# Splitting a pair's weight pieces in their order of use, with one sum formed a step earlier from raw weights

## The chip, the cores and the metric

The kernel runs on one core of a Trainium2 chip. What counts is the device time of one execution in microseconds (us), as the median of several runs. The engines carry short names here: PE (TensorE, the matmuls), PEld (its weight loads), DVE (VectorE), ACT (ScalarE), POOL (GpSimd) and SP (SyncE, which here issues the loads of the weights). Each engine works through its own stream of instructions in order, and an instruction that waits on a semaphore holds up all that stand behind it on that engine.

## The reference

The program is a two-layer trunk over 512 frames of width 1024. Cut to the products that matter here, one layer is:

```python
h = rmsnorm(x, norm1_g[i])
z = h @ w_in[i] + b_in[i]                       # q, k, v, o of the mLSTM; rq, rk, rv, rg; gates gm, gr
...
merged = jax.nn.sigmoid(gm) * (y_m @ w_bm[i]) + jax.nn.sigmoid(gr) * (y_r @ w_br[i])
x = x + merged @ w_out[i]
h2 = rmsnorm(x, norm2_g[i])
x = x + jnp.square(jax.nn.relu(h2 @ w_ff1[i] + b_ff1[i])) @ w_ff2[i] + b_ff2[i]
```

All weights are float32 in memory and each is used once, so the kernel is a stream of weights past a resident activation.

## The kernel before

**Splitting.** A float32 matmul is made of three faster ones: weights and activations are each split into a high part `h` and a low part `l`, and a product is formed as h·h + h·l + l·h (the weight's part named first: L557 weight high with activation high, L558 weight high with activation low, L559 weight low with activation high). For each piece of weights of 128 x 1024 numbers ACT makes the high part (a copy at L321) and DVE the low part (a subtraction at L322 that reads ACT's result). The row `w_B<-wr` on ACT is thus the high part of piece B, and `w_B<-wr,w_B` on DVE the low one; `wr` is the raw piece as loaded.

**Pairs.** 75 of the units of weights are "pairs": the rotary projections of the retention (`brq`, `brk`, four heads a layer), two of the four gate blocks `bgm`, the four `gr`, and most of the two feed-forward products (`f` and `o`). A pair computes a 2 x 2 block product by seven products instead of eight (Strassen's scheme in Winograd's form). Each product is 12 matmuls of 256 columns. The weights of a pair come as four pieces, each with its own high and low part:

- A holds B11 and t1, and feeds P1 and P5
- B holds B21 and t2, and feeds P6 and P2
- C holds B22 and t3, and feeds P3 and P7
- D holds t4 alone (half the width), and feeds P4

`run_pair` issues them in the order P1, P5, (P4 of the pair before), P6, P2, P3, P7; its own P4 is put off into the next unit. So the order of use is A, A, B, B, C, C, D. Three PSUM banks a, b, c collect the products: P1, P6, P7, P4 go one after the other into bank a, P5 and P3 into c, P2 into b. After each product an eviction reads the bank, and the next product into the same bank waits for it. Where the pair's result goes through `pair_tiles`, ACT evicts P1, P5, P6 and P4 (L633, L635, L639, L645), and DVE adds P2, P3 and P7 (L637, L641, L643). In the second feed-forward product `o` the evictions are DVE adds into `l0x` or `l1x` (L1554, L1556).

**Sums of the weights.** t1, t3 (and in some pairs t2 and t4) are formed beforehand by additions in DRAM, by DMAs that POOL issues (L379). 28 pairs, 14 in each layer (the brq, brk, bgm and gr pairs), have no such t2: DVE forms it as t1 + B22, from the second half of A's raw piece and the first half of C's, into the second half of B's raw buffer. This is the sum of L481. Pairs that are not "full" form t4 as well: DVE adds the two halves of B's raw piece into its own buffer (L484), and the split of D reads it there. Hence B's raw buffer is in use until D has been split.

**Order of preparation.** `PIECE` lists the pieces, and the list gives the order in which they are loaded and split. `ready(k)` calls `prep_next` until piece k is prepared, some pieces ahead of its use. `prep_next` first tops up the raw loads (`fill_raws`, on SP's queue, in order, into four buffers and one extra), then splits one piece. In program order the old list gives A, C, B, D. The sum of L481 stands behind the split of C, the sum of L484 behind the split of B. The split pieces live in a ring of three buffers (tag `w`) and D in one of its own; a split waits until the matmuls that read the buffer's last content are over. A scheduler, by priorities and by when data is due, then decides how the instructions of an engine's stream interleave, but the splits and the loads keep their order among themselves (`in_order`).

Of the kernel before, what the change touches and what calls it, by code (L numbers as in the profile page):

```python
# [38 lines left out]
OP = mybir.AluOpType  # L39
# [6 lines left out]
D = 1024  # L46
# [4 lines left out]
Q = 512  # L51
# [42 lines left out]
PRODUCTS = {"P1": ("A", 0, 0), "P5": ("A", 1, 4), "P2": ("B", 0, 2), "P6": ("B", 1, 5), "P3": ("C", 0, 6),  # L94
            "P7": ("C", 1, 3), "P4": ("D", 0, 1)}

PIECE = {"A": ("B11", "t1"), "C": ("B22", "t3"), "B": ("B21", "t2"), "D": ("t4",)}

GIVEN = ("B11", "B12", "B21", "B22")
MADE = {"t1": ("B12", "B11"), "t3": ("B12", "B22"), "t2": ("t1", "B22"), "t4": ("t2", "B21")}  # L100
# [15 lines left out]
def parts_of(u):  # L116

    return {"PAIR": list(PIECE), "WIDE": HALVES}.get(u[0], [0])

# [5 lines left out]
def is_wide(g):  # L125
    return g[1][:2] in ("rv", "rw")


def is_full(g):

    return is_gate(g) or g[0] > 0 and g[1][0] == "f"


def has_t2(g):

    return is_full(g) or g[1][0] == "f"
# [117 lines left out]
def build(ctx, tc, ins, out):  # L254
    nc = tc.nc
    ve, ac, gp, te = nc.vector, nc.scalar, nc.gpsimd, nc.tensor
    units = [u for i in range(L) for u in unit_list(i)]
# [59 lines left out]
    def tmp(name, dt=F32):  # L317
        return cur["tmp"].tile([P, T], dt, name=name, tag="t", bufs=cur["ntmp"])

    def split(src, hi_ap, lo_ap):  # L320
        a = ac.activation(hi_ap, src, AF.Copy)  # L321
        return a, ve.tensor_sub(lo_ap, src, hi_ap.bitcast(F32))  # L322

    def in_order(kind, *new):

        for a, b in zip(cur.get(kind, ()), new):
            tc.add_manual_dep(b.ins, a.ins.name, ORDER, reason="order of the weights")
        cur[kind] = new
# [4 lines left out]
    for g, v in groups().items():  # L333
        index[g] = len(index)
        src, n, w = ("wwide", 2, UN) if is_wide(g) else ("wpairs", len(v), Q)
# [7 lines left out]
    def block(g, x):  # L343
        return given[g, x] if x in GIVEN else sums[g, x]
# [54 lines left out]
    def full(n):  # L399
        return units[n][0] in ("PAIR", "WIDE") and is_full(units[n][1])  # L400

    order = [(n, x) for n, u in enumerate(units) for x in parts_of(u)]
    place = {x: k for k, x in enumerate(order)}
    loads = [(n, x) for n, x in order if full(n) or x not in ("D", ("t4", 0), ("t4", 1))]
    raws, pieces, kept = {}, {}, {}
    formed = {}

# [3 lines left out]
    def halves(n):  # L411

        return [slice(0, Q), slice(Q, UN)] if n == 1 else [slice(0, UN)]

    def fill_raws(most=RAWS + 1):
        while at["load"] < len(loads) and len(raws) + len(kept) < most:
            n, x = loads[at["load"]]
            r = None
            if n in cur["room"] and cur["more"] not in raws:
                cur["more"] = n, x  # L420
                r = cur["low"].tile([P, UN], F32, name=f"wr{at['load']}", tag="wrx", bufs=1)
            elif len(raws) - (cur["more"] in raws) >= RAWS:
                break
            raws[n, x] = r = r or wpool.tile([P, UN], F32, name=f"wr{at['load']}", tag="wr", bufs=RAWS)
            if x:
                _, g, p = units[n]
                assert made.get((g, x[1] if is_wide(g) else p)) == 2 * len(MADE_OF(g)), (g, p, made, at["unit"])
                if is_wide(g):
                    in_order("load", nc.sync.dma_start(r, block(g, x[0])[x[1]]))
                else:  # L430
                    for k, y in enumerate(PIECE[x][:1] if x == "B" and not has_t2(g) else PIECE[x]):
                        in_order("load", nc.sync.dma_start(r[:, k * Q:(k + 1) * Q], block(g, y)[p]))
            elif units[n][0] == "IF":
                eng = nc.sync if n else nc.scalar
                eng.dma_start(r[:, 0:64], ins["wif"][n * L // NU])
            else:
                w = ins["wstream"][at["whole"]]
                for c in halves(n):
                    in_order("load", nc.sync.dma_start(r[:, c], w[:, c]))
                    for k in (2, 3) if n == 1 and not c.start else ():  # L440
                        nc.sync.dma_start(cur["x0"][k], ins["xT"][k])
                at["whole"] += 1
            at["load"] += 1

    def prep_next():
        n, x = order[at["prep"]]
        at["prep"] += 1
        fill_raws()

        w = Q if x == "D" else UN  # L450
        pl = cur["last"] if n >= NU - LAST else wpool
        kw = {"tag": "d", "bufs": 1} if x == "D" else {"tag": "l", "bufs": LAST} if pl is not wpool else {
            "tag": "w", "bufs": PIECES}
        wide = isinstance(x, tuple)
        nm = f"{x[0]}{x[1]}" if wide else x
        gates = units[n][0] == "IF"
        both = pl.tile([P, 2 * w + SLACK], F32R, name=f"w{n}_{nm}", **kw)
        o = 22 if units[n][0] == "PAIR" or pl is not wpool else 0
        out_ = [both[:, o + a * w:o + a * w + w] for a in range(1 if gates else 2)]
        r = formed.pop((n, x), None)  # L460
        if r is None:
            r = raws.pop((n, x))
        if gates:
            z = out_[0]
            gp.memset(z.bitcast(F32), 0.0)
            z = z.rearrange("p (k g c) -> p k g c", g=4, c=32)
            split(r[:, 0:64].rearrange("p (k g c) -> p k g c", g=2, c=H), z[:, :, 0:2, 0:H], z[:, :, 2:4, 0:H])
        elif x == 0:
            with tc.high_priority(AHEAD if n < 10 and units[n][0] == "V" or units[n][1:] == SOON else 0):
                for c in halves(n):  # L470
                    in_order("prep", *split(r[:, c], *[a[:, c] for a in out_]))
        else:
            in_order("prep", *split(r[:, :w], *out_))
        pieces[n, x] = out_
        if full(n) or not wide and x in ("A", "C") and has_t2(units[n][1]):
            pass
        elif x == "A" or wide and x[0] == "t2":
            kept[n, x] = r
        elif x == "C":

            ve.tensor_tensor(raws[n, "B"][:, Q:], kept.pop((n, "A"))[:, Q:], r[:, :Q], OP.add)  # L481
        elif x == "B":

            ve.tensor_tensor(r[:, :Q], r[:, :Q], r[:, Q:], OP.add)  # L484
            formed[n, "D"] = r
        elif wide and x[0] == "B21":
            t = cur["br"].tile([P, UN], F32, name=f"t4{n}_{x[1]}", tag=("ph", "pl")[x[1]])
            ve.tensor_tensor(t, kept.pop((n, ("t2", x[1]))), r, OP.add)
            formed[n, ("t4", x[1])] = t

    def ready(k):
        while at["prep"] < min(len(order), k + 1):
            prep_next()
# [44 lines left out]
    def run_pair(name, act, done):  # L538
# [5 lines left out]
        def product(x):  # L544
            w, half, j = PRODUCTS[x]
            ready(place[n, "A"] + READY[x])
            wh, wl = [a[:, half * Q:(half + 1) * Q] for a in pieces[n, w]]
            b = {"P2": "b", "P5": "c", "P3": "c"}.get(x, "a")
            first = x in ("P1", "P5") or x == "P2" and "b" not in bank
            if first:  # L550
                bank[b] = own(f"{name}{b}") if x == "P2" and cur["own"] else ps(f"{name}{b}")
            o = bank[b][:, 0:S]
            for k in range(4):
                s = slice(k * P, (k + 1) * P)
                h, l = act[k](j)
                f, e = first and k == 0, k == 3
                te.matmul(o, wh[:, s], h, start=f, stop=False, skip_group_check=True)  # L557
                te.matmul(o, wh[:, s], l, start=False, stop=False, skip_group_check=True)  # L558
                cur["mm"] = te.matmul(o, wl[:, s], h, start=False, stop=e, skip_group_check=True)  # L559
            if x == "P1" and cur["own"] == "written":  # L560
                bank["b"] = own(f"{name}b")
                with ahead():
                    ac.activation(bank["b"][:, 0:S], o, AF.Copy)
            else:
                done(x, o)
            if x == "P2" and cur["own"]:
                cur["own"] = "written"
            pace()

        def last():  # L570
            product("P4")
            for w in PIECE:
                del pieces[n, w]
# [404 lines left out]
    def big(name, dt):  # L978

        return [bpool.tile([P, T], dt, name=f"{name}{k}", tag="big", bufs=KT) for k in range(KT)]  # L980

    x = big("x0", F32)
# [25 lines left out]
    for i in range(L):  # L1008
# [440 lines left out]
        for c in range(KT):  # L1449
# [4 lines left out]
            u = tmp(f"l{i}bml{c}")  # L1454
# [15 lines left out]
        if i == L - 1:  # L1470
            x_pool = phase("x", act_side)
            whole = x_pool.tile([P, KT, T], F32, name=f"l{i}x", tag="x")
            x = [whole[:, c, :] for c in range(KT)]
        else:
            x = big(f"l{i}x", F32)
# [361 lines left out]
```

## Time and profile before

| | |
|---|---|
| median of three runs | 2280.92 us (2279.55 to 2281.22) |
| the profiled execution's own time | 2280.06 us |
| its span | 2278.3 us |
| granted TensorE clock in it | 0.999 |
| DVE busy | 1747.5 us (77 %) |
| ACT busy | 1281.5 us (56 %) |

The page of a profile lists busy times by engine, the chain of work that ended last, and groups of instructions. The view of waits sums, for each engine and line, the idle time just before its instructions and names what ended it. The timeline lists single instructions with start, duration and, in square brackets, idle time with its releaser. Matmuls are pipelined: their ends are modelled (0.28 or 0.39 us each), while the next one of 256 columns starts 0.11 to 0.12 us later. So what a wait costs PE is read from the starts: the step between two starts, less that 0.11. The names of tiles have their numbers left out (`w_B` is piece B of any unit), while the listings of order below carry them: `w43_B` is piece B of unit 43.

### The profile page before, as it was taken

Reading aid. Unit: us, or ns where it says so; the run is one execution under the profiler, and the core shown is the slowest. Engines: PE = TensorE matmul, PEld = TensorE weight load, DVE = VectorE, ACT = ScalarE, POOL = GpSimd, SP = SyncE. Lnnn points to the kernel's source line nnn. Section 1 sums busy time; section 2 is a strip of 40 time slices with the busy share of each in tenths; the row PEclk is TensorE's granted clock in tenths of the full one; section 3 lists DMA queues with packets and bytes.
Section 4 is the critical chain, followed back from the end, with each engine's and each line's share of the span. In section 5 each row is a group of like instructions: output and inputs, shape, how many; then the busy total and the mean of one; then the engine's idle time right before and its main releaser. Section 6 shows DMA issues by size and latency. Waiting matters only on the chain.

```text
span 2278.3 us, 36390 instructions
## 1 busy us (share of the span) xinstructions
PE 2263.4 (99%) x13532; PEld 2009.3 (88%) x13532; DVE 1747.5 (77%) x2680; ACT 1281.5 (56%) x1881; POOL 605.5 (27%) x952
## 2 busy tenths in 40 slices
PE   9999999999999999999999999999999999999998
PEld 8888899888898899999888888998888988999997
DVE  7877777886676877787779687678867678887786
ACT  6766544654554556556557564455545546566564
POOL 3332222223124322223432322221231243111112
PEclk9999999999999999999999999999999999999999
DMA  6776887787789888888787768877877898888841
GB/s 215 189 192 176 246 224 223 222 232 216 236 231 267 222 229 228 238 238 222 227 220 197 185 178 244 240 210 223 239 216 219 248 265 217 256 239 231 249 159 60
DMA packets 185889, 499.32 MB, mean 219 GB/s; under 512 B 26400, under 2 KB 26784, under 8 KB 185712
## 3 DMA queue, kind: packets, MB, share of 16 engines
q0 software_dynamic: 57520, 188.53, 37.0%
q1 hardware_dynamic: 112496, 280.57, 36.6%
q10 hardware_dynamic: 15696, 27.91, 3.6%
q8 instruction: 106, 1.74, 0.3%
q14 instruction: 71, 0.58, 0.1%
HBM read 478.03 MB, written 194.51 MB: 295 GB/s over the span
## 4 chain that ended last, share of the span: by engine, by line
PE 90%; DVE 5%; ACT 2%; issue 1%; DMA 1%; POOL 0%; SPq 0%; DVEq 0%; ACTq 0%; POOLq 0%
PE l0f L502 2%; PE l0f L503 2%; PE l0f L504 2%; PE l0br L502 1%; PE l0br L503 1%; PE l1br L502 1%; PE l1br L503 1%; PE l1br L504 1%; PE l0br L504 1%; DVE w_B L322 1%; PE l0pg L502 1%; PE l0pg L504 1%; PE l1bm L503 1%; PE l0bm L503 1%; PE l0bm L502 1%
## 5 line engine op out<-in xcount | busy, mean ns | idle before, releaser
L322 DVE TENSOR_TENSOR w<-wr,w 128x1024 fp32r<-128x1024 f32 (+1 forms) x193 | 234.3, 1217 | 47.6 <-ACT w L321 45.3
L321 ACT ACTIVATE w<-wr 128x1024 fp32r<-128x1024 f32 (+1 forms) x193 | 199.7, 1041 | 122.3 <-issue 28.5
L321 ACT ACTIVATE w_B<-wr 128x1024 fp32r<-128x1024 f32 x123 | 130.5, 1061 | 148.5 <-PE l1bm L504 13.1
L322 DVE TENSOR_TENSOR w_B<-wr,w_B 128x1024 fp32r<-128x1024 f32 x123 | 150.2, 1222 | 52.5 <-ACT w_B L321 52.3
L321 ACT ACTIVATE w_C<-wr 128x1024 fp32r<-128x1024 f32 x75 | 79.3, 1058 | 63.4 <-issue 9.5
L322 DVE TENSOR_TENSOR w_C<-wr,w_C 128x1024 fp32r<-128x1024 f32 x75 | 92.5, 1234 | 28.6 <-ACT w_C L321 28.6
L322 DVE TENSOR_TENSOR w_A<-wr,w_A 128x1024 fp32r<-128x1024 f32 x75 | 91.7, 1223 | 15.6 <-ACT w_A L321 14.6
L321 ACT ACTIVATE w_A<-wr 128x1024 fp32r<-128x1024 f32 x75 | 79.0, 1053 | 39.6 <-DMA wr<-wpairs 8.8
L321 ACT ACTIVATE w_t<-wr 128x1024 fp32r<-128x1024 f32 x56 | 59.4, 1060 | 62.7 <-PE l0g2va L610 6.3
L321 ACT ACTIVATE w_D<-wr 128x512 fp32r<-128x512 f32 x75 | 47.3, 631 | 67.3 <-DVE wr L484 18.3
L322 DVE TENSOR_TENSOR w_t<-wr,w_t 128x1024 fp32r<-128x1024 f32 x56 | 68.3, 1222 | 21.2 <-ACT w_t L321 20.6
L502 PE MATMUL l0f<-l0n2h,w 128*128 128x512 f32 x176 | 68.8, 391 | 0.0
L503 PE MATMUL l0f<-l0n2l,w 128*128 128x512 f32 x176 | 68.7, 390 | 0.0
L504 PE MATMUL l0f<-l0n2h,w 128*128 128x512 f32 x176 | 68.6, 390 | 0.0
L322 DVE TENSOR_TENSOR w_D<-wr,w_D 128x512 fp32r<-128x512 f32 x75 | 51.7, 689 | 14.1 <-ACT w_D L321 13.7
L379 POOL DMA_DIRECT2D s30t<-wpairs x24 | 16.8, 701 | 88.7 <-PE l1o20a L559 8.7
L504 PEld LDWEIGHTS l0f<-l0n2h,w 128*128 128x128 f32 x176 | 33.1, 188 | 6.9
L502 PEld LDWEIGHTS l0f<-l0n2h,w 128*128 128x128 f32 x176 | 33.1, 188 | 6.6
L503 PEld LDWEIGHTS l0f<-l0n2l,w 128*128 128x128 f32 x176 | 33.1, 188 | 6.5
L502 PE MATMUL l1f<-l1n2h,w 128*128 128x512 f32 x96 | 37.6, 392 | 0.0
L503 PE MATMUL l1f<-l1n2l,w 128*128 128x512 f32 x96 | 37.5, 390 | 0.0
L504 PE MATMUL l1f<-l1n2h,w 128*128 128x512 f32 x96 | 37.4, 390 | 0.0
(5828 smaller groups left out, 9081.2 us busy)
## 6 DMA issues: line engine op xcount, KB each, us to landing
wr<-wstream SPq DMA_DIRECT2D x189, 512.0 KB, 5.0
wr<-wpairs SPq DMA_DIRECT2D x225, 256.0 KB, 4.0
wr<-wwide SPq DMA_DIRECT2D x48, 512.0 KB, 4.6
s3t<-wwide POOLq DMA_DIRECT2D x24, 256.0 KB, 4.3
s6t<-wwide POOLq DMA_DIRECT2D x24, 256.0 KB, 5.2
s18t<-wwide POOLq DMA_DIRECT2D x24, 256.0 KB, 5.6
s21t<-wwide POOLq DMA_DIRECT2D x24, 256.0 KB, 5.1
s24t<-wpairs POOLq DMA_DIRECT2D x24, 256.0 KB, 5.8
```

The lines of the kernel that those rows point to most:

```text
L321: a = ac.activation(hi_ap, src, AF.Copy)
L322: return a, ve.tensor_sub(lo_ap, src, hi_ap.bitcast(F32))
L379: dma = gp.dma_start(piece(g, x, p, q), piece(g, MADE[x][a], p, q), max_dma_last_dim=4096, **kw)
L502: te.matmul(o, sh, mh, start=first, stop=False)
L503: te.matmul(o, sh, ml, start=False, stop=False)
L504: cur["mm"] = te.matmul(o, sl, mh, start=False, stop=last)
```

## The change

The list `PIECE` becomes A, B, C, D, so pieces are split in the order of use. Pairs without a loaded t2 still load A, C, B; the others now load A, B, C. For the former, the sum that makes t2 moves from behind C's split to just ahead of B's split, and reads C's raw piece, which has been loaded but not yet split. Nothing is computed that was not computed before, and nothing is left out.

```diff
-PIECE = {"A": ("B11", "t1"), "C": ("B22", "t3"), "B": ("B21", "t2"), "D": ("t4",)}
+PIECE = {"A": ("B11", "t1"), "B": ("B21", "t2"), "C": ("B22", "t3"), "D": ("t4",)}
...
-    loads = [(n, x) for n, x in order if full(n) or x not in ("D", ("t4", 0), ("t4", 1))]
+    loads = []
+    for n, u in enumerate(units):
+        xs_ = parts_of(u)
+        if u[0] == "PAIR" and not has_t2(u[1]):
+            xs_ = ["A", "C", "B"]
+        loads += [(n, x) for x in xs_ if full(n) or x not in ("D", ("t4", 0), ("t4", 1))]
...
+        if x == "B" and not has_t2(units[n][1]):
+            ve.tensor_tensor(raws[n, "B"][:, Q:], kept.pop((n, "A"))[:, Q:], raws[n, "C"][:, :Q], OP.add)
...
-        if full(n) or not wide and x in ("A", "C") and has_t2(units[n][1]):
+        if full(n) or x == "C" or x == "A" and has_t2(units[n][1]):
             pass
         elif x == "A" or wide and x[0] == "t2":
             kept[n, x] = r
-        elif x == "C":
-
-            ve.tensor_tensor(raws[n, "B"][:, Q:], kept.pop((n, "A"))[:, Q:], r[:, :Q], OP.add)
```

Lines below L455 carry higher numbers afterwards: the sum of L481 is L456, the one of L484 is L488, and L637, L641, L643 are L641, L645, L647.

First place: DVE's stream around `l0r0brk` (unit 43) in layer 0, behind the split of unit 42 (`l0r0brq`). Before:

```order
L322 TENSOR_TENSOR w42_B_3099<-wr55_2940,w42_B_3099 128x1024
L484 TENSOR_TENSOR wr55_2940<-wr55_2940 128x512
L322 TENSOR_TENSOR w42_D_3121<-wr55_2940,w42_D_3121 128x512
L322 TENSOR_TENSOR w43_A_3139<-wr56_2976,w43_A_3139 128x1024
L637 TENSOR_TENSOR l0r0brqy0_3091<-l0r0brqb_3155,l0r0brqy0_3091 128x256
L322 TENSOR_TENSOR w43_C_3182<-wr57_3014,w43_C_3182 128x1024
L641 TENSOR_TENSOR l0r0brqy1_3092<-l0r0brqc_3124,l0r0brqy1_3092 128x256
L481 TENSOR_TENSOR wr61_3202<-wr59_3096,wr60_3118 128x512
L643 TENSOR_TENSOR l0r0brqy1_3092<-l0r0brqa_3103,l0r0brqy1_3092 128x256
L322 TENSOR_TENSOR w43_B_3206<-wr58_3094,w43_B_3206 128x1024
```

And now:

```order
L322 TENSOR_TENSOR w42_C_3100<-wr54_2909,w42_C_3100 128x1024
L322 TENSOR_TENSOR w42_D_3121<-wr55_2940,w42_D_3121 128x512
L456 TENSOR_TENSOR wr58_3095<-wr56_2976,wr57_3014 128x512
L322 TENSOR_TENSOR w43_A_3139<-wr56_2976,w43_A_3139 128x1024
L641 TENSOR_TENSOR l0r0brqy0_3092<-l0r0brqb_3155,l0r0brqy0_3092 128x256
L322 TENSOR_TENSOR w43_B_3183<-wr58_3095,w43_B_3183 128x1024
L645 TENSOR_TENSOR l0r0brqy1_3093<-l0r0brqc_3124,l0r0brqy1_3093 128x256
L488 TENSOR_TENSOR wr58_3095<-wr58_3095 128x512
L647 TENSOR_TENSOR l0r0brqy1_3093<-l0r0brqa_3103,l0r0brqy1_3093 128x256
L322 TENSOR_TENSOR w43_C_3207<-wr57_3014,w43_C_3207 128x1024
```

B's split has taken the place of C's, the t4 sum follows it closely and stands ahead of the eviction of P7 (L643, now L647), and the t2 sum of the next unit (into wr61) has left this stretch. The load of `w43_B` (wr58) is the load that used to wait for the release of A's raw buffer of unit 42; that release is now the split of `w42_D`, since with two pieces of a pair split it is B's buffer, still in use for t4, that is handed on. The same holds for the loads of `w44_B`, `w61_B` and their like in layer 1, and the loads behind them on SP wait with them.

Second place: DVE's stream at the split of `l0bgm2` (unit 44), the next pair. Before:

```order
L1154 SCALAR_TENSOR_TENSOR l0r0brqw1_3266<-l0r0brqy1_3092,bc0_251,l0cos_2933 128x512
L322 TENSOR_TENSOR w44_C_3316<-wr60_3118,w44_C_3316 128x1024
L1155 TENSOR_TENSOR l0r0brqu1_3265<-l0r0brqu1_3265,l0r0brqw1_3266 128x512
L322 TENSOR_TENSOR w44_B_3342<-wr61_3202,w44_B_3342 128x1024
L322 TENSOR_TENSOR l0r0ql1_3086<-l0r0brqu1_3265,l0r0qh1_3085 128x512
L484 TENSOR_TENSOR wr61_3202<-wr61_3202 128x512
```

And now:

```order
L1158 SCALAR_TENSOR_TENSOR l0r0brqw1_3266<-l0r0brqy1_3093,bc0_251,l0cos_2933 128x512
L456 TENSOR_TENSOR wr61_3203<-wr59_3097,wr60_3118 128x512
L1159 TENSOR_TENSOR l0r0brqu1_3265<-l0r0brqu1_3265,l0r0brqw1_3266 128x512
L322 TENSOR_TENSOR w44_B_3317<-wr61_3203,w44_B_3317 128x1024
L322 TENSOR_TENSOR l0r0ql1_3087<-l0r0brqu1_3265,l0r0qh1_3086 128x512
L488 TENSOR_TENSOR wr61_3203<-wr61_3203 128x512
L322 TENSOR_TENSOR w44_C_3343<-wr60_3118,w44_C_3343 128x1024
```

B keeps its row; the sum stands where C's split stood, and C's split comes behind the t4 sum.

Third place: DVE's stream at the split of `l0o10` (unit 107) in the feed-forward of layer 0. Before:

```order
L322 TENSOR_TENSOR w107_B_8975<-wr197_8843,w107_B_8975 128x1024
L484 TENSOR_TENSOR wr197_8843<-wr197_8843 128x512
L652 TENSOR_TENSOR l0f20st_8864<-l0f20st_8864 128x512
L322 TENSOR_TENSOR l0hl20_8863<-l0f20st_8864,l0hh20_8862 128x768
L653 SCALAR_TENSOR_TENSOR l0f20st_8864<-l0f20st_8864 128x256
L322 TENSOR_TENSOR w107_D_8998<-wr197_8843,w107_D_8998 128x512
L654 SCALAR_TENSOR_TENSOR l0f20st_8864<-l0f20st_8864 128x256
L1556 TENSOR_TENSOR l0x1_7211<-l0x1_7211,l0o10c_9001 128x256
L322 TENSOR_TENSOR w108_A_9016<-wr198_8866,w108_A_9016 128x1024
L1556 TENSOR_TENSOR l0x1_7211<-l0x1_7211,l0o10a_8979 128x256
```

And now:

```order
L322 TENSOR_TENSOR w107_C_8976<-wr197_8843,w107_C_8976 128x1024
L322 TENSOR_TENSOR w107_D_8998<-wr196_8780,w107_D_8998 128x512
L1560 TENSOR_TENSOR l0x1_7211<-l0x1_7211,l0o10c_9001 128x256
L656 TENSOR_TENSOR l0f20st_8864<-l0f20st_8864 128x512
L657 SCALAR_TENSOR_TENSOR l0f20st_8864<-l0f20st_8864 128x256
L322 TENSOR_TENSOR w108_A_9016<-wr198_8866,w108_A_9016 128x1024
L322 TENSOR_TENSOR l0hl20_8863<-l0f20st_8864,l0hh20_8862 128x768
L658 SCALAR_TENSOR_TENSOR l0f20st_8864<-l0f20st_8864 128x256
L1560 TENSOR_TENSOR l0x1_7211<-l0x1_7211,l0o10a_8979 128x256
```

C's split stands where B's stood, B's is five rows ahead of it (where C's was), and the eviction of P5 (L1556, now L1560, reading bank c of `l0o10`) has moved from behind the low half of `l0hl20` to ahead of L656.

## The prediction

> **What bounds the kernel.** I read the page first, then PE's waits, then the timeline at the places that these name.
>
> ```profile
> span 2278.3 us, 36390 instructions
> ...
> PE 2263.4 (99%) x13532; PEld 2009.3 (88%) x13532; DVE 1747.5 (77%) x2680; ACT 1281.5 (56%) x1881; POOL 605.5 (27%) x952
> ...
> PE 90%; DVE 5%; ACT 2%; issue 1%; DMA 1%; POOL 0%; SPq 0%; DVEq 0%; ACTq 0%; POOLq 0%
> ```
>
> PE is busy for 2263.4 of 2278.3 us, and the change takes no matmul away. Splits on DVE and ACT matter only where PE stands still for them. PE's waits, with their sum, number and longest in us, say where:
>
> ```profile
> PE l1f10a L559 <- DVE w_B L322: 0.4, 1, 0.4
> ...
> PE l0o10c L557 <- DVE l0x L1556: 0.4, 1, 0.4
> PE l0o20c L557 <- DVE l0x L1556: 0.4, 1, 0.4
> ...
> PE l1o30a L559 <- DVE w_B L322: 0.4, 1, 0.4
> PE l0o20a L559 <- DVE w_B L322: 0.4, 1, 0.4
> PE l0o10a L559 <- DVE w_B L322: 0.3, 1, 0.3
> ...
> PE l0bgm2a L559 <- DVE w_B L322: 0.3, 1, 0.3
> PE l1bgm2a L559 <- DVE w_B L322: 0.3, 1, 0.3
> PE l0o30a L559 <- DVE w_B L322: 0.2, 1, 0.2
> ```
>
> Of 75 pairs, seven wait for the low part of B, always in the third matmul of P6, the first to need it. No pair waits for C's. B is split third and used second, so the change aims at a real wait. But it is a small one. What one costs, in PE's starts at l0o10:
>
> ```profile
> 896.32 0.28 PE L558 MATMUL l0o10a<-l0hl,w_B 128*128 128x256 f32 x1
> 896.94 0.39 PE L559 MATMUL l0o10a<-l0hh,w_B 128*128 128x256 f32 x1 [0.34 <-DVE w_B L322]
> 897.16 0.28 PE L557 MATMUL l0o10a<-l0hh,w_B 128*128 128x256 f32 x1
> ...
> 900.74 0.38 PE L557 MATMUL l0o10c<-l0hh,w_C 128*128 128x256 f32 x1 [0.43 <-DVE l0x L1556]
> ...
> 902.36 0.28 PE L557 MATMUL l0o10a<-l0hh,w_C 128*128 128x256 f32 x1
> ```
>
> The steps are 0.62 and 0.22 us where undisturbed ones are 0.11, so the wait costs 0.62 in all, 0.28 more than the view's idle time. With 0.28 added to each, the seven cost 0.68 three times, 0.62, 0.58 twice and 0.48: **4.3 us**, 0.19% of the time. That is all that B's lateness can cost now.
>
> **The change, part by part.** No instruction is added or removed; sums and splits keep their durations. So the question is only who comes late next.
>
> *B ahead of C in the feed-forward pairs.* DVE at l0o10:
>
> ```profile
> 889.91 1.23 DVE L322 TENSOR_TENSOR w_C<-wr,w_C 128x1024 fp32r<-128x1024 f32 x1 [0.26 <-ACT w_C L321]
> ...
> 893.92 1.23 DVE L322 TENSOR_TENSOR l0hl<-l0f13st,l0hh 128x1024 fp32r<-128x1024 f32 x1 [1.13 <-ACT l0hh L321]
> ...
> 895.66 1.22 DVE L322 TENSOR_TENSOR w_B<-wr,w_B 128x1024 fp32r<-128x1024 f32 x1
> 896.92 0.69 DVE L484 TENSOR_TENSOR wr<-wr 128x512 f32<-128x512 f32 x1
> ...
> 901.73 0.42 DVE L1556 TENSOR_TENSOR l0x<-l0x,l0o10a 128x256 f32<-128x256 f32 x1
> ```
>
> B's low part moves to where C's was, two short rows behind 889.91, and ends at the latest where the row of 893.92 begins, 2.5 us before its use at 896.4; P6 waits no more. C takes B's place and ends near 896.9; P3 needs it two products after P6's start, 2 x 12 x 0.113 = 2.7 us later at 898.9, so C is 2 us early. The t4 sum goes with B into DVE's idle 1.13 us ahead of 893.92, of which it takes 0.60 (the next row starts 0.60 after it); without that idle time it would push l0hl's low part, and with it the queue, by 0.60, and the gain here would be nothing. P3's own wait (900.74) was for the eviction of P5, which now stands right behind D's split, ahead of l0f20st's work, and goes too. What comes last then is P7: it waits for P6's eviction, which ends at 902.15 behind an unbroken queue on DVE. Only the 0.60 of the t4 sum leaves that queue, so P7 starts some 0.6 earlier, not 1.3. I take **0.6** here and at l0o20, and the whole wait where no such queue shows among PE's waits: 0.48 at l0o30, 0.68 at l1f10 and at l1o30. Together **-3.0**.
>
> *The t2 sum just ahead of B.* At bgm2 of both layers B gains nothing. DVE and PE there:
>
> ```profile
> 323.60 1.22 DVE L322 TENSOR_TENSOR w_C<-wr,w_C 128x1024 fp32r<-128x1024 f32 x1
> ...
> 325.34 1.22 DVE L322 TENSOR_TENSOR w_B<-wr,w_B 128x1024 fp32r<-128x1024 f32 x1
> ...
> 330.54 1.22 DVE L322 TENSOR_TENSOR w<-wr,w 128x1024 fp32r<-128x1024 f32 x1
> ```
>
> ```profile
> 332.43 0.39 PE L504 MATMUL l0bm<-l0ymh,w 128*128 128x512 f32 x1
> ```
>
> The sum now begins at 323.60, where C's low part began, and ends at 324.29; ACT's high part of B (1.06) can begin only then and ends at about 325.35, so the low part starts at 325.34 as before. The 0.58 stays. DVE's queue up to the next unit's weights (330.54) gets longer by the sum (0.60) and by one eviction (0.33) now ahead of it: their low part ends at 331.76 + 0.93 = 332.7, and PE wants it at 332.43. About **+0.3** each, between 0 (other matmuls stand ahead of it) and 0.9; together +0.6.
>
> *The load that waits for D.* At l0r0brk, B's raw load used to wait for the split of unit 42's A and now waits for that of its D:
>
> ```profile
> 305.49 1.23 DVE L322 TENSOR_TENSOR w_B<-wr,w_B 128x1024 fp32r<-128x1024 f32 x1 [0.46 <-ACT w_B L321]
> ...
> 308.14 0.69 DVE L322 TENSOR_TENSOR w_D<-wr,w_D 128x512 fp32r<-128x512 f32 x1 [0.70 <-ACT w_D L321]
> ...
> 312.08 0.42 DVE L641 TENSOR_TENSOR l0r0brqy<-l0r0brqc,l0r0brqy 128x256 f32<-128x256 f32 x1
> 313.61 0.69 DVE L481 TENSOR_TENSOR wr<-wr,wr 128x512 f32<-128x512 f32 x1 [1.11 <-DMA wr<-wpairs]
> 314.22 0.42 DVE L643 TENSOR_TENSOR l0r0brqy<-l0r0brqa,l0r0brqy 128x256 f32<-128x256 f32 x1
> ```
>
> ```profile
> 308.86 0.33 SPq L432 DMA_DIRECT2D wr<-wpairs  x1
> ```
>
> ```profile
> 315.03 0.28 PE L557 MATMUL l0r0brqa<-l0xnh,w_D 128*128 128x256 f32 x1
> ```
>
> ```profile
> wr<-wpairs SPq DMA_DIRECT2D x225, 256.0 KB, 4.0
> ```
>
> With t4 formed early, D's split follows C's at 306.7 and ends at 307.4, and the load is issued. The page has a median of 4.0 us to landing; the load issued at 308.86 released the sum at 313.61, 4.75 later. So the piece is there between 311.4 and 312.2, and behind it come ACT's 1.06, DVE's low part 1.14, L641's eviction 0.33, the t4 sum 0.60 and L643 0.42, 3.6 in all: L643 ends between 315.0 and 315.8. Behind the split that waits stand just these evictions, and P4 of unit 42 needs L643: it starts at 315.03 today. P6 itself needs B's low part 1.36 (P4) and 0.23 later, at 316.6, and has it by 314.4. The cost lies between 0 and 0.9, and up to 1.9 if landing took 5.8, the longest median of the page. I take **+0.5** in each layer, halfway between the two rows: +1.0. The loads behind it on SP, those of the next pair, follow within 2 us; I cost them at nothing. The same handing on occurs at r3's brk, with more room:
>
> ```profile
> 539.30 0.42 DVE L643 TENSOR_TENSOR l0r3brqy<-l0r3brqa,l0r3brqy 128x256 f32<-128x256 f32 x1
> ```
>
> ```profile
> 541.82 0.28 PE L557 MATMUL l0r3brqa<-l0xnh,w_D 128*128 128x256 f32 x1
> ```
>
> L643 ends 2.1 us ahead of P4 there, against 0.4 at r0; cost 0 up to a landing of 5.7. At four places of the gr pairs the sum has moved ahead of an eviction, and C's raw piece is loaded only where B's split was (at l0gr1 by 655.3), since that is now the split which frees its buffer:
>
> ```profile
> 654.04 1.22 DVE L322 TENSOR_TENSOR w_B<-wr,w_B 128x1024 fp32r<-128x1024 f32 x1
> ...
> 661.30 0.42 DVE L643 TENSOR_TENSOR l0gr1y<-l0gr1a,l0gr1y 128x256 f32<-128x256 f32 x1
> ```
>
> ```profile
> 663.43 0.28 PE L557 MATMUL l0gr1a<-l0xnh,w_D 128*128 128x256 f32 x1
> ```
>
> The eviction ends 1.7 ahead of its P4 and the sum takes 0.6 of that, so this costs 0 up to a landing of some 6 us.
>
> [...]
>
> *Sum.* -3.0 + 0.6 + 1.0 = **-1.4**, from the profiled execution's own 2280.06 (span 2278.3 and 1.8 around it) to 2278.7. The median before lies 0.86 above that execution, so I forecast a median of **2279.5**.
>
> **Rivals.** A measurement of this kernel can tell about 0.2% from no change, 4.6 us: below 2276.4 is faster, above 2285.5 slower.
>
> 1. *The gain is given back.* DVE has 77% of the span, and a piece split earlier pushes evictions later; P7's queue at l0o10 is one case. With the gain at nothing and the costs as above, +1.6: about 2282.5. For it: two of the waits quoted are for evictions already. Against: nothing at l0o30, l1f10 and l1o30 shows such a queue.
> 2. *Slower: raw loads land late.* B's buffer is held until D's split, and SP's queue stands behind it. With a landing of L us, r0's two sites cost L - 3.9 each, r3's two L - 5.7, gr's four L - 6. Beside -3.0 + 0.6 this passes +4.6 from L = 6.3 on; at 6.5 it is +6.4, about 2287. Against it: medians of 4.0 and the single 4.75.
> 3. *Faster.* All 4.3 of B and P3's two waits of 0.7 each go, with no cost: -5.7, about 2275.2. Against it: bgm2's sum and P7's queue.
>
> That the order does not in fact change is excluded by the listings: DVE's rows of B and C have changed places.
>
> **How the numbers follow.** Forecast 0.50 (its own range 2276.4 to 2281.5), given back 0.27, slower 0.13, faster 0.10. The first two lie within 0.2%: same 0.77. The range that leaves out 2 in 10 ends just beyond the 0.2% on both sides, 2276.0 to 2285.6.
>
> **What would show it.** Right: no wait for w_B at o10, o20, o30, l1f10 and l1o30, the two at bgm2 still there; P7 of l0o10 near 901.7; at l0r0brk a new wait of P4 for L647 below 1 us, with ACT's high part of B released by a DMA. Wrong: waits for w_C at P3, or ACT idle for several us for `wr<-wpairs` in many pairs, or PE's waits together shrinking by more than 4 us.

## The result, and the profile after

| | before | after |
|---|---|---|
| median, same chip | 2281.06 us (2277.6 to 2286.08, 9 runs) | 2286.63 us (2282.31 to 2292.35, 9 runs) |
| ratio | | 1.0024, 95% interval 1.0015 to 1.0032 |
| profiled execution, own time | 2280.06 us | 2287.14 us |
| its span, mean granted clock | 2278.3 us, 0.999 | 2285.4 us, 0.997 |

The change makes the kernel slower, by 0.24%. PE does the same matmuls, so the 7.1 us between the two spans are time in which PE stood still or ran slower. The page of the changed kernel, its busy times and its chain of waits by engine:

```profile
span 2285.4 us, 36441 instructions
...
PE 2265.3 (99%) x13532; PEld 2010.7 (88%) x13532; DVE 1743.8 (76%) x2680; ACT 1277.3 (56%) x1881; POOL 605.9 (27%) x952
...
PE 89%; DVE 6%; ACT 2%; issue 2%; DMA 1%; POOL 0%; DVEq 0%; ACTq 0%; SPq 0%; POOLq 0%
```

DVE is less busy than before, and yet has a larger share of the chain: it is late, not full. PE's waits in the changed kernel (sum, number and longest in us):

```profile
PE l0r0brqa L561 <- DVE l0r0brqy L647: 2.4, 1, 2.4
PE l1bgm3a L561 <- DVE l1bgm3y L647: 2.4, 1, 2.4
...
PE l1gr0a L561 <- DVE l1gr0y L647: 0.6, 1, 0.6
PE l0gr0a L561 <- DVE l0gr0y L647: 0.6, 1, 0.6
```

Five of the seven waits for `w_B` are gone, those of o10, o20, o30, l1f10 and l1o30. Of the two at bgm2 that of layer 1 stays at 0.4 us; that of layer 0 shrinks to 0.12 in this trace. In their place P4 waits for L647, the eviction of P7, at four places. The first of the two largest is at `l0r0brk`. DVE's timeline there (start, duration, in brackets the idle time before and what ended it):

```profile
309.42 0.42 DVE L641 TENSOR_TENSOR l0r0brqy<-l0r0brqb,l0r0brqy 128x256 f32<-128x256 f32 x1
314.68 1.23 DVE L322 TENSOR_TENSOR w_B<-wr,w_B 128x1024 fp32r<-128x1024 f32 x1 [4.83 <-ACT w_B L321]
315.82 0.42 DVE L645 TENSOR_TENSOR l0r0brqy<-l0r0brqc,l0r0brqy 128x256 f32<-128x256 f32 x1
316.15 0.68 DVE L488 TENSOR_TENSOR wr<-wr 128x512 f32<-128x512 f32 x1
316.75 0.42 DVE L647 TENSOR_TENSOR l0r0brqy<-l0r0brqa,l0r0brqy 128x256 f32<-128x256 f32 x1
```

DVE stands still for 4.83 us ahead of B's low part. It waits for ACT's high part, which in turn stood still; ACT and SP there:

```profile
308.06 0.38 ACT L643 ACTIVATE l0r0brqy<-l0r0brqa 128x256 f32<-128x256 f32 x1
313.58 1.06 ACT L321 ACTIVATE w_B<-wr 128x1024 fp32r<-128x1024 f32 x1 [5.14 <-PE l0r0brka L563]
```

```profile
307.00 0.80 SPq L437 DMA_DIRECT2D wr<-wpairs  x2
```

In the kernel before, SP asked for this piece 11 us earlier, and it was in place by 299.8, long before its split began at 312.51:

```profile
295.85 0.33 SPq L432 DMA_DIRECT2D wr<-wpairs  x1
```

In the changed kernel the view names PE as what ended ACT's 5.14 us, but the matmul named had long been done: what came last is the raw piece, requested at 307.00 (the first of the two issues in that row) and in place at 313.48 by the trace's end of that transfer. L645 and L647 stand behind B's low part though neither needs it. And the standstill has a second price. PE's starts behind it, and the granted clock in windows of 2 us (PE's busy time and its instructions, clock, DMA share, GB/s):

```profile
314.55 0.28 PE L563 MATMUL l0r0brkc<-l0xsh,w_A 128*128 128x256 f32 x1
317.22 0.39 PE L561 MATMUL l0r0brqa<-l0xnh,w_D 128*128 128x256 f32 x1 [2.40 <-DVE l0r0brqy L647]
...
318.99 0.41 PE L563 MATMUL l0r0brqa<-l0xnh,w_D 128*128 128x256 f32 x1
319.20 0.41 PE L561 MATMUL l0r0brka<-l0xsh,w_B 128*128 128x256 f32 x1
```

```profile
314.00:316.00 2.00, 0.82 (x8) 1.00 1.10 285
316.00:318.00 2.00, 0.78 (x6) 1.00 0.83 277
318.00:320.00 2.00, 2.00 (x12) 0.54 0.03 12
320.00:322.00 2.00, 2.00 (x13) 0.61 0.45 131
322.00:324.00 2.00, 2.00 (x20) 1.00 0.83 264
```

From 318.2 to 321.6 the matmuls start every 0.21 us instead of 0.113: half clock for 3.4 us, which costs 1.7. The same follows the standstill at `l1bgm3`. There it is another DVE instruction that waits for a transfer, the moved t2 sum:

```profile
1492.87 0.69 DVE L456 TENSOR_TENSOR wr<-wr,wr 128x512 f32<-128x512 f32 x1 [5.05 <-DMA wr<-wpairs]
1493.48 0.42 DVE L641 TENSOR_TENSOR l1bgm3y<-l1bgm3b,l1bgm3y 128x256 f32<-128x256 f32 x1
...
1494.95 0.42 DVE L645 TENSOR_TENSOR l1bgm3y<-l1bgm3c,l1bgm3y 128x256 f32<-128x256 f32 x1
1495.28 0.41 DVE L647 TENSOR_TENSOR l1bgm3y<-l1bgm3a,l1bgm3y 128x256 f32<-128x256 f32 x1
```

It forms t2 of the next pair, and ahead of the evictions of this one. Before, the sum ran at 1482.98 with its pieces in place, ahead of an L643 at 1486.69:

```profile
1482.98 0.69 DVE L481 TENSOR_TENSOR wr<-wr,wr 128x512 f32<-128x512 f32 x1
...
1486.69 0.42 DVE L643 TENSOR_TENSOR l1bgm3y<-l1bgm3a,l1bgm3y 128x256 f32<-128x256 f32 x1
```

### The profile page after: what moved, and what is told of

Read it like the earlier page. It is cut to its first block, busy times and chain, and to the rows that moved or that the text cites. A ratio compares the mean times of both kernels' runs of the same rounds, so it can differ in the third digit from the quotient of the medians.

```text
span 2285.4 us, 36441 instructions
## 1 busy us (share of the span) xinstructions
PE 2265.3 (99%) x13532; PEld 2010.7 (88%) x13532; DVE 1743.8 (76%) x2680; ACT 1277.3 (56%) x1881; POOL 605.9 (27%) x952
## 4 chain that ended last, share of the span: by engine, by line
PE 89%; DVE 6%; ACT 2%; issue 2%; DMA 1%; POOL 0%; DVEq 0%; ACTq 0%; SPq 0%; POOLq 0%
PE l0f L506 2%; PE l0f L507 2%; PE l0f L508 2%; PE l0br L506 1%; PE l1br L507 1%; PE l1br L506 1%; PE l0br L507 1%; PE l0br L508 1%; PE l1br L508 1%; PE l1f L506 1%; PE l1f L507 1%; PE l1f L508 1%; DVE w_B L322 1%; PE l0bm L508 1%; PE l0pg L506 1%
```

## The experiments

Three theories. **L** (late loads): raw pieces of the 28 pairs without a loaded t2 come late, a DVE instruction waits for them, and evictions stand behind it. **Q** (queue): the new order of splits, sums and evictions costs by itself, whatever the loads do. **N**: the difference is a matter of the clock or of chance. Ratios are against the kernel before on the same chip, with 95% intervals.

**1 and 2. Half of the change each.** The new order for those pairs that load t2 (most of `f` and `o`), as in this diff, and for the 28 others, with `not has_t2(g)`:

```diff
+def new_order(g):
+    return has_t2(g)
...
+    pair = ["A", "B", "C", "D"] if u[0] != "PAIR" or new_order(u[1]) else ["A", "C", "B", "D"]
```

> The new order A, B, C, D only for the pairs with a loaded t2 (all f and o pairs); the 28 brq, brk, bgm and gr pairs keep A, C, B, D and their sum. In the changed kernel's trace the projections lose 4.6 us in layer 0 and 6.3 in layer 1 against before, and the feed-forward stretches gain 1.2 and 2.8. Late loads (theory L: in pairs without t2 raw pieces are requested later, DVE waits for their landing, evictions stand behind, PE's P4 waits): the loads of the projections are as before, so the loss goes and the gain stays, 2281 - 4 = about 2277. Queue order (theory Q: splits and the t4 sum placed earlier hold up evictions, wherever it is done): the f and o pairs lose as well, at or above 2281. Chance (theory N: the after runs only had a lower granted clock): no difference of more than 2 us from before.

> The counterpart: the new order and the moved sum only for the 28 pairs without t2, the f and o pairs as before. Theory L: all of the loss without the gain, 2281 + 9 to 11 = 2290 to 2292, with PE waits at P4 for the eviction of P7 in r0's brk or bgm3. Theory Q: a part of the loss in proportion to the pairs, 28 of 75, so about +2. Theory N: within 2 us of before.

The first: 2276.55 us (11 runs), ratio 0.9989 (0.9980 to 0.9998). The second: 2287.91 us, ratio 1.0039 (1.0027 to 1.0052), with these waits of PE (its line numbers are 8 higher):

```profile
PE l0r0brqa L569 <- DVE l0r0brqy L655: 2.4, 1, 2.4
PE l1o10c L569 <- ACT l1hh L327: 1.8, 1, 1.8
PE l1gr2a L569 <- DVE l1gr2y L655: 1.2, 1, 1.2
```

The wait at l1o10c lies in a pair that keeps the old order, and stays unexplained. The change is a gain of some 2.5 us and a loss of some 9, in different pairs. N falls: the two halves lie apart by far more than either interval.

**3 and 4. Two attempts on the waiting, both misses.** One hands the extra raw buffer on only when it is free, so that B's load at `l0r0brk` is early again; the other forms the t2 sum on POOL.

```diff
+            held = cur["more"] and (cur["more"][1] == "B" and (cur["more"][0], "D") in formed or cur["more"] in kept)
-            if n in cur["room"] and cur["more"] not in raws:
+            if n in cur["room"] and cur["more"] not in raws and not held:
```

```diff
-            ve.tensor_tensor(raws[n, "B"][:, Q:], kept.pop((n, "A"))[:, Q:], raws[n, "C"][:, :Q], OP.add)
+            gp.tensor_tensor(raws[n, "B"][:, Q:], kept.pop((n, "A"))[:, Q:], raws[n, "C"][:, :Q], OP.add)
```

> The changed kernel, but the extra raw buffer is handed to a new load only when it is really free (not while it holds the sum for D or is kept for the t2 sum). The load of l0r0brk's B then waits for the split of A again, as before the change, and so do its like; the order of splits and sums stays that of the changed kernel. Theory L: the 2.4 us wait of P4 at l0r0brk goes, with most of layer 0's 4.6; the wait at l1bgm3, where the sum needs C's raw piece, stays: 2281 to 2283, 4 to 5 below the changed kernel. Theory Q: no change against the changed kernel, 2286.

> The changed kernel with the t2 sum on POOL instead of DVE, so that a sum waiting for C's raw piece no longer stands ahead of evictions on DVE; B's split still waits for it. Theory L: the 2.4 us wait at l1bgm3 (sum ahead of L641, L645, L647, itself waiting 5 us for a load) goes, the one at l0r0brk stays: 2 to 3 us below the changed kernel, 2283 to 2284, if POOL's longer sum costs nothing at B's split. Theory Q: the DVE queue is shorter by 28 x 0.6 us, a gain of at most 1 us; 2285 to 2286.

Third: 2285.74 us, ratio 1.0031 (1.0019 to 1.0042). B's load is early (295.58), but another now comes late: the t2 sum of the next pair, ahead of B's split, waits 5.33 us for its piece, and P4 at `l0r0brq` waits 3.5. The wait has moved by one instruction. Fourth: 2290.06 us, ratio 1.0053 (1.0040 to 1.0065). The wait at `l1bgm3` is gone. At `l0r0brk` B's load is as late as in the changed kernel, and P4 waits 2.5 us; at `l1r0brk` B's split now waits for POOL's sum, and P4 2.2.

**5, 6 and 7. Order and lateness apart.** The fifth keeps the new order but forms the t2 sum right behind A's split. That frees A's raw buffer a step earlier, so B's load at `l0r0brk` is early (295.46), and the sum of the next pair, which waits for a transfer, stands behind this pair's evictions. The sixth gives the 28 pairs their old order A, C, B, D but holds the raw pieces as long as the change does, so that loads are as late. The seventh is the fifth with the third's way of handing on.

```diff
-        if x == "B" and not has_t2(units[n][1]):
-            ve.tensor_tensor(raws[n, "B"][:, Q:], kept.pop((n, "A"))[:, Q:], raws[n, "C"][:, :Q], OP.add)
...
-        elif x == "A" or wide and x[0] == "t2":
+        elif x == "A":
+            ve.tensor_tensor(raws[n, "B"][:, Q:], r[:, Q:], raws[n, "C"][:, :Q], OP.add)
+        elif wide and x[0] == "t2":
```

```diff
+    return has_t2(g)
...
+    pair = ["A", "B", "C", "D"] if u[0] != "PAIR" or new_order(u[1]) else ["A", "C", "B", "D"]
...
-            ve.tensor_tensor(raws[n, "B"][:, Q:], kept.pop((n, "A"))[:, Q:], raws[n, "C"][:, :Q], OP.add)
+            ve.tensor_tensor(raws[n, "B"][:, Q:], kept.pop((n, "A"))[:, Q:], kept.pop((n, "C"))[:, :Q], OP.add)
...
+        if x == "C" and not has_t2(units[n][1]):
+            kept[n, "C"] = r
```

> The changed kernel, order A, B, C, D in all pairs, but the t2 sum is formed right behind A's split, as soon as C's raw piece is there, so that A's raw buffer is free one step earlier. The load of l0r0brk's B then waits for A's split as before the change, and in DVE's stream the next unit's sum stands behind L647 instead of ahead of it; B's split, the t4 sum and the evictions stand as in the changed kernel. Theory L (DVE waits for a raw piece that is requested late, and evictions stand behind it): no wait of P4 at l0r0brk, 2 to 5 us below the changed kernel, 2278 to 2282 where before has 2278.5; at bgm3 the next unit's sum still stands ahead of L641 to L647 and can wait there. Theory Q (the order of splits and evictions itself): P4 at l0r0brk waits as in the changed kernel, no gain, 2284 to 2286.

> The f and o pairs in the new order (as in the first experiment), the 28 others split in the old order A, C, B, D, but with the sum formed at B's step, one step later, so A's and C's raw buffers are both held until then. The loads are then released as late as in the changed kernel (l0r0brk's B by the split of unit 42's D), but B is split third, behind the evictions L641 and L643. Theory L needs both, a late load and a piece wanted early with evictions behind it: the wait at l0r0brk is gone or below 0.5 us, total within 3 us above the first experiment, 2276 to 2280. If late loads alone are the cause (more transfers at once, whoever waits), it loses like the second experiment: 2284 to 2288.

> The fifth experiment (sum right behind A's split) with the hand-out of the extra raw buffer of the third. The load of l0r0brk's B waits for A's split in both, but here the scheduler puts unit 44's sum, which waits for the load of unit 44's C (released by D's split of unit 42), ahead of w43_B's split and of L645, L647 in DVE's stream; in the fifth it stood behind them. Theory L: the sum begins only when that load has landed, at about 313 to 315, L647 ends near 317, and P4 at l0r0brk waits 2 to 3.5 us again: 2 to 5 us slower than the fifth, 2280 to 2283 where before has 2279. Theory Q, or buffers alone: like the fifth, 2277 to 2278.

Fifth: 2277.71 us, ratio 0.9993 (0.9985 to 1.0002). Sixth: 2275.77 us, ratio 0.9983 (0.9974 to 0.9992). Seventh: 2284.44 us, ratio 1.0015 (1.0006 to 1.0024). DVE at `l0r0brk` in the fifth, sixth and seventh, the sum or split that waits and the eviction of P7 (L647, L655, L648):

```profile
312.62 0.42 DVE L647 TENSOR_TENSOR l0r0brqy<-l0r0brqa,l0r0brqy 128x256 f32<-128x256 f32 x1
314.71 0.69 DVE L483 TENSOR_TENSOR wr<-wr,wr 128x512 f32<-128x512 f32 x1 [1.67 <-DMA wr<-wpairs]
```

```profile
312.23 0.42 DVE L655 TENSOR_TENSOR l0r0brqy<-l0r0brqa,l0r0brqy 128x256 f32<-128x256 f32 x1
314.38 1.23 DVE L328 TENSOR_TENSOR w_B<-wr,w_B 128x1024 fp32r<-128x1024 f32 x1 [1.72 <-ACT w_B L327]
```

```profile
315.99 0.69 DVE L484 TENSOR_TENSOR wr<-wr,wr 128x512 f32<-128x512 f32 x1 [5.90 <-DMA wr<-wpairs]
...
318.67 0.42 DVE L648 TENSOR_TENSOR l0r0brqy<-l0r0brqa,l0r0brqy 128x256 f32<-128x256 f32 x1
```

All three wait for a transfer that lands between 313 and 316. In the fifth and sixth the eviction stands ahead of the instruction that waits, and PE loses nothing there; in the seventh it stands behind, and P4 waits 4.1 us. So B's late load alone costs nothing here (the sixth has it, requested at 308.57), and the new order alone costs little (the fifth has it): Q falls in its plain form, and L holds with a condition. The wait costs where evictions stand behind it. What Q keeps is a wait of 0.7 us at `gr0` of each layer, which the fifth has too. The sixth beats both kernels; from the first, at 0.9989, it can't be told apart.

**8 and 9. Why the loads are late.** The changed kernel again, and the same with POOL's additions in DRAM paused around the two `r0`:

```diff
+        if at["unit"] in (42, 43, 182, 183):
+            return
```

> The changed kernel unchanged, on the chip and beside the runs of the kernel before that the other experiments use, for a comparison in one place and a second trace. 5 to 6 us above before, about 2285, if its loss lies in the program; the wait of P4 at l0r0brk for L647 of some 2.4 us again, with the raw load landing at about 313.5 however early it was issued; the one at l1bgm3 may differ, since it hung on one load that took 8 us.

> The changed kernel with one thing moved on POOL: the DMAs that form later weights' sums in DRAM pause during units 41 and 42 of each layer and are caught up afterwards; DVE's stream around l0r0brk and the release of its raw load are those of the changed kernel. If the late landing of that load (6.5 to 7.1 us after issue, near 313.5 to 314, however early it is issued) comes from those sums, three of which POOL issues at 304 to 307: it lands 4.0 to 4.8 us after its issue at 307, near 311.5, and P4's wait at l0r0brk falls from 2.4 to 3.0 us to below 0.7, as the prediction's term had it. If the five loads that SP issues within 3 us are enough, or something else, the landing stays above 6 us and the wait above 2.

Eighth: 2284.97 us (11 runs), ratio 1.0022 (1.0013 to 1.0031), the result once more. In the changed kernel POOL issues three additions just then:

```profile
304.39 0.80 POOL L379 DMA_DIRECT2D s4t<-wwide  x1 [2.98 <-PE l0bm L508]
305.67 0.79 POOL L379 DMA_DIRECT2D s4t<-wwide  x1 [0.48 <-PE l0r0brqa L563]
307.02 0.80 POOL L379 DMA_DIRECT2D s4t<-wwide  x1 [0.56 <-PE l0r0brqc L563]
```

The raw piece B of `l0r0brk`, by start and end of its transfer in each trace in which it is late:

| kernel | requested | landed | took |
|---|---|---|---|
| after | 307.00 | 313.48 | 6.48 |
| the sixth | 308.57 | 313.18 | 4.61 |
| the eighth | 306.94 | 314.03 | 7.09 |
| the ninth, additions paused | 307.11 | 309.69 | 2.58 |

With the additions in flight, a request 1.6 us earlier gained nothing: the piece landed about when the last of them did (313.83 in the profile after, 312.55 in the sixth, 313.97 in the eighth). In the profile before, where B's piece was early, the load of 308.86 is that of the next pair's C, and it too landed at 313.49, behind additions that landed by 312.85. With the additions paused B's piece took 2.58 us, against 4.61 to 7.09 with them in flight, and P4's wait at `l0r0brq` was gone.

The time of the ninth did not fall all the same: 2284.93 us (2280.41 to 2290.28), ratio 1.0027 (1.0017 to 1.0037). The profiled execution is its fastest run, and only that one has a trace. So the pause shows what delays the piece, and not what the kernel would gain without that delay. What its other runs lost is open; the paused additions must run later, and a raw load at 318.99 in that trace took 10.6 us, where the same load took 5.6 in the profile after.

**10, 11 and 12. The clock.** To see whether the half clock comes from the standstill, matmuls of ones were put on PE between P5 of `l0r0brk` and P4 of `l0r0brq`, first in bank c (in which the sums of `l0r0brk` come out changed), then in bank b, which is free; between them the changed kernel as it is.

```diff
+        if site:
+            bank["b"] = ps(f"{name}b")
+            for _ in range(10):
+                f = te.matmul(bank["b"][:, 0:P], ones, ones, start=True, stop=True, skip_group_check=True)
...
```

> The changed kernel with 12 matmuls of ones, whose result nothing reads, put on PE between P5 of l0r0brk and P4 of l0r0brq, where PE stands still for 2.4 us in the profile after; nothing else is added or moved. From the 26 rows of the warm-up at the start (4.61 us at the lower rate, half of that at full rate) the 12 should take about 2.1 to 2.3 us. Theory G (the standstill itself makes the granted clock fall to a half afterwards, as at 318 to 322 us in the profile after): PE is busy while L647 is late, P4 starts where it did (near 317.2 plus or minus the scatter of the landing), the windows of 1 us after it show a clock of 1.00, and the 1.7 us of half clock there are gone, while a stall and its half clock at l1bgm3 may stay. The median falls by 1 to 1.7 us against the changed kernel beside it, hardly more than the scatter, so the windows decide. Rival H (the clock falls because of something else at that place, such as the burst of evictions and splits): the windows behind P4 still show 0.5 for 3.4 us. Theory L alone, with no part for the clock: no change of the median, and PE's start of P6 of l0r0brk stays where it is, near 319.2.

> The changed kernel itself on the same chip, as the measure for the one with the filled standstill: ratio 1.002 to 1.0025 against the kernel before. Theory G: wherever a wait of P4 of 2 us or more stands among PE's waits, windows of 1 us behind it show either 1.00 throughout or a half clock for 3.4 us in all, nothing between, and a place without such a wait shows none.

> As the run before it, but with 10 matmuls of ones in bank b of l0r0brk, which is free then (P2 starts it afresh later), so that they wait for nothing; the result is the reference's. By the 24 rows of the run before, which took 2.7 us, they take 2.25 us right behind P5 of l0r0brk and nearly fill the standstill of 2.4 to 3.0 us seen there in four profiles of the changed kernel. They cost nothing, since P4 of l0r0brq waits for L647 anyhow. Theory G (PE's standstill makes the granted clock fall afterwards): P4 waits less than 1 us, starts between 317.2 and 317.8 as in those profiles, the windows behind it show 1.00 for certain, and the median falls by up to 1.7 us in the runs where the clock would have fallen there, so by some 1 us in the mean: 2284 to 2285.5 against the 2285 to 2286.6 of the changed kernel. Rival H (the clock falls for another reason at that place): half clock for 3.4 us behind P4 all the same. Theory L without a part for the clock: P6 of l0r0brk starts near 319.2, as in the profile after, instead of at P4's start and 1.4 us.

The tenth is a miss: its matmuls waited for the eviction of bank c, which itself stands behind B's split on ACT, so PE stood still for 2.23 us and then worked 2.7 us for nothing. No half clock followed. 2287.11 us, ratio 1.0044 (1.0031 to 1.0058). The eleventh: 2285.66 us, ratio 1.0032 (1.0021 to 1.0042); P4 waited 2.8 us, and 3.4 us of half clock followed. The twelfth, PE and the clock:

```profile
314.61 2.39 PE L587 MATMUL l0r0brkb<-ones_r 128*128 128x128 f32 x20
317.42 0.39 PE L562 MATMUL l0r0brqa<-l0xnh,w_D 128*128 128x256 f32 x1 [0.41 <-DVE l0r0brqy L659]
...
318.92 0.28 PE L562 MATMUL l0r0brka<-l0xsh,w_B 128*128 128x256 f32 x1
```

```profile
316.00:318.00 2.00, 1.59 (x13) 1.00 0.83 285
318.00:320.00 2.00, 2.00 (x20) 1.00 0.02 8
320.00:322.00 2.00, 2.00 (x20) 1.00 0.45 147
```

L647 (here L659) is as late as ever, but the clock stays full and P6 starts at 318.92, though P4 began 0.2 us later than in the profile after. The mean clock was 0.999 in 9 of its 11 runs, and in 4 of the 27 runs of the changed kernel (those of the result, the eighth and the eleventh). That is a hint and no more, since the profiled run of the eighth has 0.998 with no half clock amid its work. The time itself, 2285.06 us, ratio 1.0027 (1.0018 to 1.0036), can't be told from the changed kernel's: the half clock is the smaller part of the loss.

## Why the prediction was wrong

The steps at which PE falls behind, from the difference of its starts against the profile before, in us:

| place | predicted | after | 8th | 11th | 12th |
|---|---|---|---|---|---|
| P4 of l0r0brq, for L647 | +0.5 | 2.6 | 3.2 | 3.0 | 2.8 |
| half clock behind it | 0 | 1.7 | 0 | 1.7 | 0 |
| the two bgm2 | +0.6 | 0.5 | 0.8 | 0.5 | 0.8 |
| P4 of the two gr0 | 0 | 1.5 | 1.6 | 1.5 | 1.6 |
| P4 of l1r0brq | +0.5 | 0 | 0 | 0 | 0.9 |
| P4 of l1bgm3 | 0 | 2.5 | 0.8 | below 0.5 | 0.9 |
| half clock behind it | 0 | 1.7 | 0 | 0 | 0 |
| P4 of l1gr2 | 0 | below 0.5 | 1.3 | 1.2 | 1.1 |
| sum | +1.6 | 10.5 | 7.7 | 7.9 | 8.1 |
| the spans differ by | -1.4 | 7.1 | 4.9 | 4.2 | 4.8 |

The rest, -2.8 to -3.7, is the gain in the feed-forward and smaller steps, among them two new losses that no term held: 0.5 at P3 of l1gr0 in all four, and 1.0 to 1.3 at P6 of l0o31 in the first three. Each column is a single execution.

- **The gain was right.** The five waits went. Forecast -3.0; the new order in `f` and `o` alone gave a ratio of 0.9989, which is -2.5 us, between -4.6 and -0.5.
- **The step that failed is the load that waits for D.** "So the piece is there between 311.4 and 312.2" took a median of 4.0 us, and one row of 4.75, and counted from the new request. But that row, the load of the next pair's C, ran behind POOL's additions: requested at 308.86, it landed at 313.49, after the last of them (312.85). Asked for at 307.00, B's piece met the same additions and came at 313.48. With the prediction's own 3.6 us behind it, L647 would end at 317.1; it ended at 317.17. The mechanism, the chain behind it and its lengths were right. The duration was wrong, and with it a term of +0.5 that measured 2.6 to 3.2. The second rival's price, L - 3.9, gives 2.6 for the 6.48 that L came to, just past its point of 6.3. Its total for that L, +6.2, lies near the 7.1 of the spans, but that is luck: of its eight sites only r0 of layer 0 cost in that trace what it said.
- **Places costed at nothing.** At `l1bgm3` the moved sum waits for the raw piece C of the next pair with this pair's evictions behind it; the prediction followed B's late load and C's at the gr pairs, not this one. At `gr0` no load is late: L647 now stands directly behind a low part (1.14) that used to stand ahead of the eviction before it, and P4 is 0.75 later in each layer. Layer 1's `r0`, where +0.5 was forecast, cost nothing in three of the four traces.
- **bgm2 was right.** Forecast +0.3 each. P4 of the two starts 0.9 later than the products around it, but PE has other matmuls meanwhile, and what it keeps of that is 0.1 to 0.4.
- **What no term held: the clock.** Without its 3.4 us the profile after would stand 3.7 above the one before. The other traces of the same order show waits that come and go from run to run, so the sizes at `l1bgm3`, `l1gr2` and `l1r0brq` belong to single executions.

The test named in the prediction, a wait of P4 for L647 below 1 us, did its work: the wait was there, at 2.4.

## What to carry to other kernels

When an instruction that waits for a transfer is moved ahead in the stream of an engine that works in order, count what now stands behind it: here evictions that PE needs, which a late piece of weights delayed without having to do with them. Read a landing against the traffic around it (here 313.2 to 314.0 for requests from 306.94 to 308.57), not as the request plus a median; and ask of each raw piece not only when it is used but when its buffer comes free. Where such a wait can't be removed, put the evictions ahead of it, as the fifth and sixth kernels do.

## What was not expected of the hardware

**Half clock after a standstill of 1.8 to 4.1 us.** In the traces of the changed kernel and of its variants PE stood still 12 times for 1.8 us or more amid its work. Eight of these were followed by half clock, seven times for 3.4 us in all (1.4 to 1.7 lost) and once, behind 4.1 us, for 6.8 (of which PE worked 5.9, some 2.9 lost); four were not, of 2.23, 2.40, 2.72 and 3.02 us. The shortest that was is 1.8 us (`l1o10c` in the second kernel). Over the whole span, the profiles before and after and the traces of the eighth to the twelfth have no such stretch without a standstill ahead of it, apart from the first 8 and the last 9 us; at the end PE waits for the closing norm (0.9 and 0.8 us in the profile after).

In the profile after the granted clock changes at 4.13, 318.16, 321.57, 1495.76 and 1499.17: the last four lie 92, 93, 437 and 438 steps of 3.413 us behind the first. Counted in these steps, its two standstills, of 2.40 and 2.38 us, each lie within one step (314.74 to 318.16 and 1492.34 to 1495.76), and the step behind it is the one at half clock; PE's next longest wait amid its work is 0.7 us (`l0o31a`). An estimate for three other traces takes the same steps and counts back from the fall of the clock near the end, at 2275.22 in the eighth, 2278.56 in the tenth and 2277.36 in the twelfth. By it the standstills of 3.02 us in the eighth and of 2.23 in the tenth, behind which the clock stayed full, are divided by the edge of a step, into 1.21 and 1.80 and, at 315.90, into 0.51 and 1.72. In the twelfth the step from 314.69 to 318.11 holds the place of the standstill, of which the matmuls of ones left 0.41 us, and the clock stayed full. Each of these is a single execution, and the runs show when the clock falls, not why.

**A DMA that takes longer the earlier it is asked for.** One transfer of 256 KB landed at nearly the same instant, 313.2 to 314.0, whether requested at 306.94 or at 308.57; with the additions in DRAM paused it took 2.58 us.
